# Prompt attention by key-value group: probabilities and values as high and low parts, value products on the full array in place of fp32 products on 64 columns

## The chip, the cores and the metric

One core of a Trainium2 chip runs the whole program. The metric is the device time of one execution in microseconds. Runs of a kernel agree within a few tenths of a per cent most of the time.

## What is computed

One step of a decoder layer: adaLN-modulated norm, one input projection, then a sparse attention (three branches) beside a state-space layer, an output projection and a gated FFN, for a prompt of 1024 tokens and 8 sample sequences of 4 tokens with a cache. The part that matters here is the prompt's attention, by chunks of 128 queries, with 8 query heads of 64 dimensions in two key-value groups of four heads. With 1024 tokens the selected branch keeps all 16 blocks, so it is plain causal attention:

```python
p_c = masked_softmax(s_c, m_c)                                  # compressed keys, at most 64 here
o_c = jnp.einsum('bqgrc,bcgd->bqgrd', p_c.astype(v_cmp.dtype), v_cmp)
...
o_s = jnp.einsum('bqgrn,bqgnd->bqgrd', p_s.astype(v_sel.dtype), ...)   # selected blocks
o_w = jnp.einsum('bqgrw,bwgd->bqgrd', p_w.astype(kv_win.dtype), kv_win[:, :, 1])   # window of 512
o = g[..., 0:1] * o_c + g[..., 1:2] * o_s + g[..., 2:3] * o_w
```

All inputs and outputs are fp32. The kernel gets fp32 accuracy in most of its products from splitting an operand into a high part, rounded to fp32r (a matmul format of its own), and a low part, the difference.

## The kernel before

The program is written as phases that open and close pools of tiles, and a scheduler decides from the data dependences, and from a simulation of its own, in which order each engine's instructions stand. Two tiles of one pool and tag share storage, and a tag's count of buffers says how many can be alive. Of PSUM, the accumulator of TensorE, the attention (`phase_attend`, L1003) holds eight banks: four for scores (tag "s", two of two banks), two for transposes ("t"), one for outputs ("o") and one for filler work ("f").

Stages, by time in the trace: adaLN loads up to 43 us; the input projections in fp32r high and low parts (`project`, L927) up to 251; the sample path, the key compression (L494, L516) and the state scan on VectorE (L1526 to L1529) up to 476; then the prompt attention by chunks in the order 4, 0, 6, 1, 7, 2, 5, 3 up to 967; the output projection (`mix_product`, L1718) up to 1088, with the products of row tiles 8 and 7 already within chunk 5; the FFN (L1800, L1843) to the end.

A chunk has two branches (0: all keys up to the chunk; 1: the window of at most five key tiles), and in each two units of four heads, (0, 1, 4, 5) and (2, 3, 6, 7), so a unit has two heads of each key-value group. `attend_scores` writes a head's scores (L1195, L1196, the mask at L1199), VectorE takes the row maximum (L1203, L1211), ScalarE the exponential (L1205, L1212). `attend_values` goes through the unit's key tiles and calls `pv_tile` for each: four transposes of 128 × 128 into a bank of tag "t" (L1269), one copy out of it, by ScalarE and VectorE in turn (L1271), and one fp32 product for each key-value group with 64 columns of values stationary and 256 columns moving (L1273). A product in fp32 is two instructions. The output of both units lies in one bank (group 0 in partitions 0 to 63, group 1 in the rest). `attend_out` copies it (L1280), transposes it (L1283) and multiplies it with the gates (L1288, L1290, then GpSimd L1291). The compressed branch goes through `pv_tile` twice per chunk with 64 rows of values.

Fillers stand between the units by a table (`PLAN`, `between`, L1029): state-space kernels and outputs, the GLU, the second half of the adaLN, the output weights (`out_weights`). They use the bank "f". The second half of the sample path (`sample_attend`) is taken up by four of its steps at chunk 4. `mix_product` uses bank "f" for the row tiles of `MIX` (8 and 7) and "t", "o", "f" for the others; its tiles come from the pool "wo", which `out_weights` opens at chunk 5. Each row tile has 48 products of 512 columns.

In the sample path `sample_load` keeps eight tiles of the cache (256 columns by four, tag "s_raw"), two runs of four. `ada_block` holds three adaLN weight tiles of 1 MB (four contraction rows by 512 columns); the projection's weights have three pairs of half matrices (tag "bw"). `kv_block` writes the projected values into the tile vst in fp32 by one ScalarE copy.

## Time and profile before

| what | value |
|---|---|
| runs timed | 1857.51, 1838.06, 1839.6 us; median 1839.6 |
| profiled execution | 1847.22 us, of which the span of the instructions is 1845.4 us |
| mean clock granted to TensorE | 0.975 of full speed |
| busy: TensorE, VectorE, ScalarE, GpSimd | 95%, 52%, 34%, 23% of the span |
| memory traffic | 143.88 MB read, 25.46 MB written |

PE is TensorE's matmul side, PEld its loading of stationary operands (which overlaps), DVE is VectorE, ACT ScalarE, POOL GpSimd, SP the engine that issues most DMAs. Busy times are sums of the instructions' durations; matmuls overlap, so a matmul's duration is longer than the distance to the next. A group's "idle before" is the time in which the engine stood still ahead of its instructions, with the instruction that ended it. All stage times below are microseconds from the start of the span.

### The profile page before, as it was taken

How to read it: one execution, taken by the hardware profiler on the slowest of the kernel's cores; microseconds unless marked ns; L12 is line 12 of the kernel's file. 1: busy time of each engine (PE TensorE's matmuls, PEld its weight loads, DVE VectorE, ACT ScalarE, POOL GpSimd, SP SyncE). 2: the span in 40 equal slices, each digit the busy share in tenths (PEclk: the TensorE clock that was granted, in tenths of full speed). 3: DMA queues.
4: the chain of work that ended last, by engine and by line, in shares of the span. 5: the costliest groups of instructions: out<-in, count | busy, mean ns of one | idle time of the engine just before them, and what ended most of it. 6: DMA issues, size and time to landing. Idle time of an engine off the chain costs nothing.

```text
span 1845.4 us, 29371 instructions
## 1 busy us (share of the span) xinstructions
PE 1745.5 (95%) x11546; PEld 1454.5 (79%) x11546; DVE 957.5 (52%) x2310; ACT 631.6 (34%) x1267; POOL 425.4 (23%) x817
## 2 busy tenths in 40 slices
...
GB/s 281 96 105 100 74 138 133 218 142 158 77 143 63 55 142 225 144 53 117 43 57 149 92 92 46 69 23 46 69 24 46 69 23 46 69 24 46 52 46 140
DMA packets 132699, 172.43 MB, mean 93 GB/s; under 512 B 17176, under 2 KB 92312, under 8 KB 132304
## 3 DMA queue, kind: packets, MB, share of 16 engines
...
q14 instruction: 48, 0.39, 0.1%
q10 hardware_dynamic: 128, 0.04, 0.0%
HBM read 143.88 MB, written 25.46 MB: 92 GB/s over the span
## 4 chain that ended last, share of the span: by engine, by line
PE 82%; DVE 8%; DMA 5%; ACT 3%; issue 2%; POOL 1%; SPq 0%; DVEq 0%; ACTq 0%; POOLq 0%
PE gu L1800 18%; PE dn L1843 13%; PE g L1800 5%; PE u L1800 4%; PE cp L516 4%; PE aso L1273 4%; PE as L1195 2%; PE ss L823 2%; PE as L1196 1%; PE q0p L927 1%; PE kv1p L927 1%; PE q1p L927 1%; PE ct L494 1%; PE u1p L927 1%; PE ada L226 1%
## 5 line engine op out<-in xcount | busy, mean ns | idle before, releaser
L1800 PE MATMUL gu<-h2h,wh 128*128 128x352 f32 x704 | 228.1, 324 | 5.0 <-ACT h2h L860 5.0
L1800 PE MATMUL gu<-h2h,wl 128*128 128x352 f32 x704 | 227.4, 323 | 0.0
L1800 PE MATMUL gu<-h2l,wh 128*128 128x352 f32 x704 | 227.0, 323 | 0.0
L1849 DVE TENSOR_TENSOR acc<-acc,dn 128x512 f32<-128x512 f32 x144 | 98.9, 687 | 229.9 <-PE dn L1843 229.9
L1808 POOL TENSOR_TENSOR al<-fa,ah 128x352 fp32r<-128x352 f32 (+1 forms) x66 | 69.5, 1053 | 415.7 <-ACT ah L1807 409.7
L1803 ACT ACTIVATE fa<-gu 128x352 f32<-128x352 f32 x44 | 20.4, 465 | 412.9 <-PE gu L1800 412.9
L1843 PE MATMUL dn<-dh,ah 128*128 128x512 f32 x352 | 141.4, 402 | 3.9 <-DVE fin L1852 3.4
L1843 PE MATMUL dn<-dl,ah 128*128 128x512 f32 x352 | 139.7, 397 | 0.0
L1843 PE MATMUL dn<-dh,al 128*128 128x512 f32 x352 | 139.2, 396 | 0.0
L1800 PEld LDWEIGHTS gu<-h2h,wh 128*128 128x128 f32 x704 | 132.7, 188 | 7.9 <-ACT h2h L860 5.3
L1800 PEld LDWEIGHTS gu<-h2l,wh 128*128 128x128 f32 x704 | 133.2, 189 | 3.8
L1800 PEld LDWEIGHTS gu<-h2h,wl 128*128 128x128 f32 x704 | 132.9, 189 | 3.1
L409 ACT CAST wh<-wr 128x1024 fp32r<-128x1024 f32 x44 | 46.0, 1048 | 151.5 <-PE g L1800 77.0
L1806 DVE TENSOR_TENSOR fa<-fa,gu 128x352 f32<-128x352 f32 x44 | 22.9, 521 | 143.9 <-ACT fa L1803 143.9
L1195 PE MATMUL as<-kst,aqA 128*128 128x320 f32 (+4 forms) x192 | 76.5, 402 | 9.0 <-ACT ap L1212 3.7
L1843 PEld LDWEIGHTS dn<-dh,ah 128*128 128x128 f32 x352 | 66.8, 190 | 22.5 <-ACT wh L409 7.5
L410 DVE TENSOR_TENSOR wl<-wr,wh 128x1024 fp32r<-128x1024 f32 x44 | 58.8, 1339 | 49.0 <-ACT wh L409 49.0
L1843 PEld LDWEIGHTS dn<-dl,ah 128*128 128x128 f32 x352 | 66.7, 189 | 15.9
L1843 PEld LDWEIGHTS dn<-dh,al 128*128 128x128 f32 x352 | 67.0, 190 | 8.4
L1196 PE MATMUL as<-kst,aqB 128*128 128x320 f32 (+4 forms) x192 | 65.6, 346 | 6.3 <-ACT aqB L1158 6.3
L1211 DVE TENSOR_REDUCE asm<-as 128x1 f32<-128x640 f32 (+3 forms) x64 | 58.7, 920 | 19.2 <-PE as L1199 18.4
L1212 ACT ACTIVATE ap<-as,asm 128x640 f32<-128x640 f32 (+3 forms) x64 | 55.9, 874 | 36.0 <-DVE asm L1211 22.6
...
## 6 DMA issues: line engine op xcount, KB each, us to landing
...
```

The costliest lines, as they stand in the source:

```text
L410: self.nc.vector.tensor_tensor(lo, raw, hi.bitcast(F32), op=ALU.subtract)
L516: nc.tensor.matmul(P[:, 256 * ab:256 * ab + 256], w[:, 8 * ab + 2 * j + i, :], x[:, i, :], start=j == 0 and i == 0 and n == 0 and ab == 0, ...
L927: nc.tensor.matmul(p[:, t, :n], h[:, k, tok], ww[:, k % 4, :n], start=m == 0, stop=m == 23)
L1195: nc.tensor.matmul(Sv, qA[:, h, :], kk, start=True, stop=False)
L1196: nc.tensor.matmul(Sv, qB[:, h, :], kk, start=False, stop=not mt)
L1211: nc.vector.tensor_reduce(mx[:, :1], Sv, axis=ax, op=ALU.max, negate=True)
L1212: nc.scalar.activation(Pv, Sv, AF.Exp, bias=mx[:, :1], accum_out=l[:, h:h + 1])
L1273: nc.tensor.matmul(O[64 * g:64 * g + 64, 256 * hf:256 * hf + 256], V[:n, 64 * g:64 * g + 64], pT[:, 256 * g:256 * g + 256], start=first, s ...
L1800: nc.tensor.matmul(gu[i], w[:, k, :], h[:, k, 352 * n:352 * n + 352], start=m == 0, stop=m == 23)
L1808: nc.gpsimd.tensor_tensor(al[:, cols], a[:, :w], ah[:, cols].bitcast(F32), op=ALU.subtract)
L1843: nc.tensor.matmul(p, a[:, sl], w[:, c], start=m == 0, stop=m == 5)
L1849: nc.vector.tensor_tensor(o, o, p, op=ALU.add)
```

## The change

The units of a branch become the two key-value groups (heads 4g to 4g+3) in place of two heads of each. For a unit's key tile `pv_turn` transposes the four heads' probabilities into a bank as before, then copies them as fp32r (high part, ScalarE) and subtracts that from the bank (low part, VectorE). The values are kept as high and low part per group beside each other, 128 columns, so one product of 128 stationary and 512 moving columns gives the product with the high values in one half of the partitions and that with the low values in the other; it is made for the high and for the low probabilities. They are issued two key tiles after the transposes. `pv_join` adds the two halves (a ScalarE copy, a VectorE addition). The compressed branch transposes the probabilities of two heads at once (they share 128 rows), and makes eight products of 256 columns with the values at rows 0 to 63 or 64 to 127 of a tile that is zero elsewhere.

The values' two parts are written by two GpSimd operations for each of eight value blocks (16 in all). PSUM in the attention: four banks "s", three "t", one "o"; the fillers use "t". The pool "wx", which now holds the work tiles of `mix_product`, opens only after the attention's pools are closed. The adaLN weights come in tiles of half the size (four of them, in place of three), the projection's weights in quarter matrices (five pairs, in place of three of halves), the sample path keeps six cache tiles in place of eight, loads them one by one, and writes the next run's scores after the values' products and not before. In `ssm_input` seven more small loads for each of four groups replace a copy.

```diff
-            wt = pool.tile([128, 4, 512], F32, tag="wada", name=f"wada{nb}_{kk}", bufs=3)
-            nc.sync.dma_start(wt, w[:, 4 * kk:4 * kk + 4, nb * 512:(nb + 1) * 512])
+            wts = [pool.tile([128, 2, 512], F32, tag="wada", name=f"wada{nb}_{kk}{i}", bufs=4) for i in range(2)]
+            for i, wt in enumerate(wts):
+                nc.sync.dma_start(wt, w[:, 4 * kk + 2 * i:4 * kk + 2 * i + 2, nb * 512:(nb + 1) * 512])
...
-        self.vst = kv.tile([128, NT, 2, 128], F32, name="vst")
...
+        self.vst = kv.tile([128, NT, 2, 4, 64], F32R, name="vst")
...
-        self.bw = self.open("bw", bufs=3)
+        self.bw = self.open("bw", bufs=5)
...
+            O = self.sample_pv(S, self.raws.pop(run), self.kvn[:, br, 1] if last else None, B, sb, nm)
+            self.own_group(R[br][:, j], O)
+            self.sample_load(sb, 4)
             if half == 0 and k < 4:
                 p = self.sample_scores(runs[k + 1], sb)
-            O = self.sample_pv(S, self.raws.pop(run), self.kvn[:, br, 1] if last else None, B, sb, nm)
-            self.own_group(R[br][:, j], O)
-            self.sample_load(sb)
...
+    def sample_load(self, sb, n):
+
...
+            raw = sb.tile([128, 4, 256], F32, tag="s_raw", name=f"s_raw{br}{b}_{j}", bufs=6)
...
         nm = f"kv{br}_{t2}"
-        vt = pb.tile([128, 2, 128], F32, tag="bk", name=nm + "v") if br == 0 else self.vst[:, 2 * t2:2 * t2 + 2, br - 1, :]
+        vt = pb.tile([128, 2, 128], F32, tag="bk", name=nm + "v")
         nc.scalar.copy(vt, p[:, :, 128:256])
+        if br:
+            v = vt.rearrange("p t (g d) -> p t g d", g=2)
+            slots = self.vst[:, 2 * t2:2 * t2 + 2, br - 1]
+            nc.gpsimd.tensor_copy(slots[:, :, 0:4:3], v)
+            nc.gpsimd.tensor_tensor(slots[:, :, 1:3], v, slots[:, :, 0:4:3].bitcast(F32), op=ALU.subtract)
...
-        self.psum("psc", s=2, t=2, o=1, f=1)
+        self.psum("psc", s=2, t=3, o=1)
...
+        self.wx = self.open("wx", bufs=2)
...
-            tags, self.tags = self.tags, "ff"
+            tags, self.tags = self.tags, self.XT
...
+        self.vch = pc.tile([128, 2, 4, 64], F32R, name="vch", bufs=1)
+        nc.gpsimd.memset(self.vch.bitcast(F32), 0.0)
+        for e in range(2):
+            rows = slice(64 * e, 64 * e + 64)
+            v = self.vcp[rows].rearrange("p (g d) -> p g d", g=2)
+            slots = self.vch[rows, e]
+            nc.gpsimd.tensor_copy(slots[:, 0:4:3], v)
+            nc.gpsimd.tensor_tensor(slots[:, 1:3], v, slots[:, 0:4:3].bitcast(F32), op=ALU.subtract)
...
-        for h in (2 * hf, 2 * hf + 1, 4 + 2 * hf, 5 + 2 * hf):
+        for h in range(4 * grp, 4 * grp + 4):
...
         k0, nk = self.attend_keys(c, br)
-        if hf == 0:
-            st["O"] = self.ps("o", f"aso{c}{br}")
-        O, att, l = st["O"], st["att"], st[br]
+        O, att, l = self.ps("o", f"aso{c}{br}{grp}"), st["att"], st[br]
         g = self.gz[:, c].rearrange("p (h b) -> p b h", b=3)
-        for t in range(nk):
-            self.pv_tile([P[:, t * 128:t * 128 + 128] for P in Ps], self.vst[:, k0 + t, br, :], O, hf, pc, f"as{c}{br}{t}", t == 0, t == nk - 1)
-        st["between"](2 * br + hf)
-        if hf == 0:
+        late = []
+        for t in range(nk + 2):
+            if t < nk:
+                late.append(self.pv_turn([P[:, t * 128:t * 128 + 128] for P in Ps], pc, f"as{c}{br}{grp}{t}"))
+            if t > 1:
+                V = self.vst[:, k0 + t - 2, br, 2 * grp:2 * grp + 2].rearrange("p a d -> p (a d)")
+                for n, x in enumerate(late.pop(0)):
+                    nc.tensor.matmul(O, V, x, start=t == 2 and n == 0, stop=t == nk + 1 and n == 1)
+        if grp == 0:
+            st["ot"] = pc.tile([128, 512], F32, tag="aot", name=f"as{c}{br}ot")
+        self.pv_join(st["ot"], O, grp, pc, f"as{c}{br}{grp}")
+        st["between"](2 * br + grp)
+        if grp == 0:
             return
         nc.vector.reciprocal(l, l)
         nc.vector.tensor_tensor(l, l, g[:, 1 + br], op=ALU.mult)
-        self.attend_out(O, l, att, pc, f"as{c}{br}", br == 0)
+        self.attend_out(st["ot"], l, att, pc, f"as{c}{br}", br == 0)
         if br == 0:
             return
-        O = self.ps("o", f"aco{c}")
-        for i in range(2):
-            self.pv_tile([st["pcb"][:, h, :] for h in (2 * i, 2 * i + 1, 4 + 2 * i, 5 + 2 * i)], self.vcp, O, i, pc, f"ac{c}", True, True)
-        self.attend_out(O, st["lc"], att, pc, f"ac{c}", False)
+
+        pcb = st["pcb"]
+        hl = self.pv_turn([pcb[:, 2 * r:2 * r + 2, :].rearrange("p h n -> p (h n)") for r in range(4)], pc, f"ac{c}")
+        ot = pc.tile([128, 512], F32, tag="aot", name=f"ac{c}ot")
+        for grp in range(2):
+            O = self.ps("o", f"aco{c}{grp}")
+            Ov = O.rearrange("p (r e q) -> p e r q", r=2, e=2)
+            for e in range(2):
+                V = self.vch[:, e, 2 * grp:2 * grp + 2].rearrange("p a d -> p (a d)")
+                for n, x in enumerate(hl):
+                    nc.tensor.matmul(Ov[:, e], V, x[:, 256 * grp:256 * grp + 256].rearrange("p (r q) -> p r q", r=2),
+                                     start=e == 0 and n == 0, stop=e == 1 and n == 1, skip_group_check=True)
+            self.pv_join(ot, O, grp, pc, f"ac{c}{grp}")
+        self.attend_out(ot, st["lc"], att, pc, f"ac{c}", False)
         t = pc.tile([128, 512], F32, tag="aot", name=f"attq{c}")
         self.norm_rows(att.rearrange("p h d -> p (h d)"), t, 1.0, self.xc_d[c * 128:(c + 1) * 128, :512], f"attn{c}", "a")
...

-    def pv_tile(self, Ps, V, O, hf, pc, name, first, last):
-
-        nc = self.nc
-        n = Ps[0].shape[-1]
-        pT = pc.tile([128, 512], F32, tag="apT", name=f"{name}pT{hf}", bufs=3)[:n]
-        p = self.ps_t(f"{name}pt{hf}")[:n]
+    def pv_turn(self, Ps, pc, name):
+
+        nc = self.nc
+        p = self.ps_t(name + "pt")
         for r in range(4):
             nc.tensor.transpose(p[:, r * 128:r * 128 + 128], Ps[r], self.ident)
-        self.flip = not self.flip
-        (nc.scalar.copy if self.flip else nc.vector.tensor_copy)(pT, p)
-        for g in range(2):
-            nc.tensor.matmul(O[64 * g:64 * g + 64, 256 * hf:256 * hf + 256], V[:n, 64 * g:64 * g + 64], pT[:, 256 * g:256 * g + 256],
-                             start=first, stop=last)
-
-    def attend_out(self, O, coef, att, pc, name, first):
-
-        nc = self.nc
-        ot = pc.tile([128, 512], F32, tag="aot", name=name + "ot")
-        nc.scalar.copy(ot, O)
+        h, lo = (pc.tile([128, 512], F32R, tag="apT" + x, name=f"{name}pT{x}", bufs=3) for x in "hl")
+        nc.scalar.copy(h, p)
+        nc.vector.tensor_tensor(lo, p, h.bitcast(F32), op=ALU.subtract)
+        return h, lo
+
+    def pv_join(self, ot, O, grp, pc, name):
+
+        nc = self.nc
+        own, other = slice(64 * grp, 64 * grp + 64), slice(64 - 64 * grp, 128 - 64 * grp)
+        nc.scalar.copy(ot[own], O[other])
+        nc.vector.tensor_tensor(ot[own], ot[own], O[own], op=ALU.add)
+
+    def attend_out(self, ot, coef, att, pc, name, first):
+
+        nc = self.nc
...
-        us = sp.tile([8, 8, 128], F32, tag="q4", name=f"us{Q}")
-        nc.vector.memset(us[:, 0:4], 0.0)
-        nc.sync.dma_start(us[:, 4:8], self.zs_d.rearrange("(b t) f -> b t f", t=4)[:, :, 1304 + 128 * Q:1432 + 128 * Q])
-        ur = sp.tile([128, 8, 8, 16], F32, tag="q4", name=f"ur{Q}")
+        usr = sp.tile([8, 8, 8, 16], F32, tag="q4", name=f"usr{Q}", bufs=3)
+        nc.vector.memset(usr[:, :, 0:4], 0.0)
+        for g in range(8):
+            f = 1304 + 128 * Q + 16 * g
+            nc.sync.dma_start(usr[:, g, 4:8], self.zs_d.rearrange("(b t) f -> b t f", t=4)[:, :, f:f + 16])
...
-            self.g1 = wo.tile([128, 1024], F32, tag="g1", name=f"g1_{tt}", bufs=1)
+            self.g1 = wx.tile([128, 1024], F32, tag="g1", name=f"g1_{tt}", bufs=1)
...
-            p = self.ps("t" if last else "f", f"{nm}xt{k2}")
+            p = self.ps("t", f"{nm}xt{k2}")
...
-            M = self.ps("of"[hf] if last else "f", f"{nm}M{hf}")
+            M = self.ps("ot"[hf], f"{nm}M{hf}")
```

Both kernels' instruction orders on TensorE, at the places that matter. First the middle of a unit of chunk 6, branch 0 in before (as601pT is the transposed tile 1 of that branch, as603pt the bank of tile 3, ap the heads' probabilities, aso the output bank):

```order
L1273 MATMUL aso_8335<-as601pT_8345,vst 64x256 x2
L1269 MATMUL as603pt_8364<-ident,ap_7940 128x128
L1269 MATMUL as603pt_8364<-ident,ap_7950 128x128
L1269 MATMUL as603pt_8364<-ident,ap_7960 128x128
L1269 MATMUL as603pt_8364<-ident,ap_7970 128x128
L1273 MATMUL aso_8335<-as602pT_8354,vst 64x256 x2
```

In the order after the change, the same place (as6002 is tile 2 of the first group, pTh and pTl its high and low part; L1211, L1212 and L1215 write the scores of a head of the next group, as L1195, L1196 and L1199 in before):

```order
L1244 MATMUL aso_8527<-as6002pTh,vst 128x512
L1244 MATMUL aso_8527<-as6002pTl,vst 128x512
L1300 MATMUL as6005pt<-ident,ap_8121 128x128
L1300 MATMUL as6005pt<-ident,ap_8131 128x128
L1300 MATMUL as6005pt<-ident,ap_8141 128x128
L1300 MATMUL as6005pt<-ident,ap_8151 128x128
L1211 MATMUL as_8517<-kst,aqA_8097 128x512
L1212 MATMUL as_8517<-kst,aqB_8098 128x512
L1211 MATMUL as_8517<-kst,aqA_8097 128x384
L1212 MATMUL as_8517<-kst,aqB_8098 128x384
L1215 LDWEIGHTS identb
L1215 MATMUL as_8517<-mk,identb 128x128
```

Two products of 64 columns per turn (one for each group of values) became two of 128 columns (one for each part of the probabilities), and they stand two tiles behind their transposes, with scores of the next group between the turns.

Second, TensorE at the hand-over from the compression to the attention, before (sc, pcT, imp and oc are the sample path's scores, transposed probabilities, importance and output over compressed keys; s240kt to s270kt transposes of cache keys, aqt the transposed queries, as the first scores of chunk 4):

```order
L676 MATMUL sc_6822<-kcT,qblk 32x128 x4
L820 MATMUL s240kt<-ident,s_raw_0_5634 128x128 x4
L820 MATMUL s250kt<-ident,s_raw_0_5636 128x128 x4
L686 MATMUL pcT_6835<-ident,s_pc_6827 128x128
L820 MATMUL s260kt<-ident,s_raw_0_5638 128x128 x4
L1153 MATMUL aqt_6798<-ident,aqhl_6793 128x128 x8
L820 MATMUL s270kt<-ident,s_raw_0_5640 128x128 x4
L691 MATMUL imp_6839<-kc,s_pcT_6837 128x30
L1195 MATMUL as_6957<-kst,aqA_6796 128x320
L695 MATMUL imp_6843<-s_y_6841,kc 128x30
L1196 MATMUL as_6957<-kst,aqB_6797 128x320
L1195 MATMUL as_6957<-kst,aqA_6796 128x320
...
L713 MATMUL oc_6858<-vc,s_pcT_6837 32x128 x4
```

and after (L1211 is the first score, as L1195 in before; sn and ss are scores of the sample path's new and cached keys):

```order
L679 MATMUL sc_6940<-kcT,qblk 32x128 x4
L689 MATMUL pcT_6953<-ident,s_pc_6945 128x128
L694 MATMUL imp_6957<-kc,s_pcT_6955 128x30
L698 MATMUL imp_6961<-s_y_6959,kc 128x30
L716 MATMUL oc_6976<-vc,s_pcT_6955 32x128 x4
L722 MATMUL sn_6985<-knT,qblk 128x64
L820 MATMUL s240kt<-ident,s_raw_0_5717 128x128 x4
L1169 MATMUL aqt_6910<-ident,aqhl_6905 128x128 x8
L823 MATMUL ss_6995<-s240kT,qblk 32x512
L820 MATMUL s250kt<-ident,s_raw_0_5719 128x128 x4
L820 MATMUL s260kt<-ident,s_raw_0_5790 128x128 x4
L1211 MATMUL as_7075<-kst,aqA_6908 128x320
```

The sample path's products from sc to oc stood with other work between them and now stand one behind the other; the transposes of cache keys and queries follow them.

Third, TensorE in chunk 5, before (mx8M is the accumulator of the output projection of row tile 8, woh and wol the parts of its weights, mx8Xh and mx8Xl those of its input):

```order
L1273 MATMUL aso_10849<-as500pT_10850,vst 64x256 x2
L1269 MATMUL as501pt_10860<-ident,ap_10683 128x128
L1269 MATMUL as501pt_10860<-ident,ap_10693 128x128
L1269 MATMUL as501pt_10860<-ident,ap_10703 128x128
L1269 MATMUL as501pt_10860<-ident,ap_10713 128x128
L1269 MATMUL as502pt_10869<-ident,ap_10683 128x128
L1269 MATMUL as502pt_10869<-ident,ap_10693 128x128
L1269 MATMUL as502pt_10869<-ident,ap_10703 128x128
L1269 MATMUL as502pt_10869<-ident,ap_10713 128x128
L1718 MATMUL mx8M_11688<-woh,mx8Xh_11674 32x512
L1718 MATMUL mx8M_11688<-woh,mx8Xl_11675 32x512
L1718 MATMUL mx8M_11688<-wol,mx8Xh_11674 32x512
```

and the first place at which mx8 stands after the change (aco, ac3otp: the compressed branch of chunk 3, the last):

```order
L1266 MATMUL aco_12123<-ac3pTh,vch 128x2x128
L1266 MATMUL aco_12123<-ac3pTl,vch 128x2x128
L1318 MATMUL ac3otp<-ident,ac3ot 128x128 x4
L1741 MATMUL mx8xt_12178<-ident,mx8xc 128x32 x4
L1741 MATMUL mx8xt_12187<-ident,mx8xc 128x32 x4
L1753 MATMUL mx8M_12197<-woh,mx8Xh_12183 32x512
L1753 MATMUL mx8M_12225<-woh,mx8Xh_12183 32x512
L1753 MATMUL mx8M_12197<-woh,mx8Xl_12184 32x512
L1753 MATMUL mx8M_12197<-wol,mx8Xh_12183 32x512
```

The products of row tile 8 stood between the tiles of chunk 5 and now stand behind the last chunk; those of row tile 7 follow them.

## Rows read from the trace of the kernel before

**Rows 1.** The page's first part: busy time and share of the span.
```profile
PE 1745.5 (95%) x11546; PEld 1454.5 (79%) x11546; DVE 957.5 (52%) x2310; ACT 631.6 (34%) x1267; POOL 425.4 (23%) x817
```

**Rows 2.** The page's chain that ended last, shares of the span by engine.
```profile
PE 82%; DVE 8%; DMA 5%; ACT 3%; issue 2%; POOL 1%; SPq 0%; DVEq 0%; ACTq 0%; POOLq 0%
```

**Rows 3.** Windows: length, busy us of PE, PEld, DVE, ACT, POOL, clock, DMA.
```profile
0.00:480.00 480.00, 440.21 (x3492) 380.22 (x3493) 326.27 (x1203) 212.82 (x408) 173.71 (x262) 0.97 0.45 145
480.00:574.30 94.30, 87.04 (x706) 56.69 (x704) 81.30 (x301) 53.39 (x130) 14.60 (x18) 0.96 0.24 76
574.30:697.00 122.70, 105.83 (x995) 73.84 (x994) 69.51 (x128) 56.22 (x134) 48.78 (x86) 0.87 0.38 111
697.00:850.00 153.00, 142.46 (x924) 89.06 (x922) 94.63 (x148) 92.22 (x198) 47.82 (x170) 0.98 0.40 136
850.00:967.00 117.00, 108.42 (x687) 68.72 (x686) 61.01 (x97) 53.03 (x122) 20.28 (x66) 0.99 0.17 58
967.00:1088.00 121.00, 112.40 (x560) 96.38 (x560) 60.26 (x93) 46.62 (x91) 27.73 (x124) 0.96 0.37 120
```
**Rows 4.** TensorE's longest waits, 490 to 990 us: total, times, longest.
```profile
PE Y L1598 <- DMA ssm_W<-K: 5.9, 1, 5.9
```

**Rows 5.** TensorE's timeline in chunk 6: start, duration, instruction.
```profile
600.88 0.66 PE L1269 MATMUL as603pt<-ident,ap 128*128 128x128 f32 x4
601.46 0.65 PE L1273 MATMUL aso<-as602pT,vst 128*64 128x256 f32 x4
...
604.38 0.66 PE L1269 MATMUL as606pt<-ident,ap 128*128 128x128 f32 x4
```

**Rows 6.** TensorE's timeline in the compression, transposes between fp32r products.
```profile
461.66 0.60 PE L494 MATMUL ct<-ident,cxr 128*128 128x128 f32 x4
462.01 0.36 PE L516 MATMUL cp<-cXl,w1hv 128*128 128x256 f32 x1
462.21 0.28 PE L516 MATMUL cp<-cXh,w1lv 128*128 128x256 f32 x1
462.33 0.28 PE L516 MATMUL cp<-cXh,w1hv 128*128 128x256 f32 x1
```

**Rows 7.** TensorE's timeline in the FFN, fp32r products of 512 columns.
```profile
1299.63 0.40 PE L1843 MATMUL dn<-dh,ah 128*128 128x512 f32 x1
1299.86 0.39 PE L1843 MATMUL dn<-dh,al 128*128 128x512 f32 x1
```

**Rows 8.** Windows of one line: L1269 (PE, PEld), L1271 (DVE, ACT), L1280 (ACT).
```profile
476.00:1008.00 532.00, 98.28 (x592) 66.38 (x592) 0.95 0.31 102
...
476.00:1008.00 532.00, 50.74 (x74) 43.16 (x74) 0.95 0.31 102
...
476.00:1008.00 532.00, 14.02 (x24) 0.95 0.31 102
```
**Rows 9.** Groups of instructions, 476 to 1008 us, by shape: busy us, mean ns.
```profile
L1211 DVE TENSOR_REDUCE asm<-as 128x1 f32<-128x640 f32 x40 | 32.7, 819 | 12.8 <-PE as L1199 12.1
...
L1157 DVE CAST aqB<-aqt 64x512 fp32r<-64x512 f32 x16 | 10.9, 684 | 5.3 <-ACT aqA L1156 5.0
...
L1156 ACT CAST aqA<-aqt 128x512 fp32r<-128x512 f32 x16 | 9.4, 586 | 7.4 <-PE aqt L1153 7.3
...
L1158 ACT CAST aqB<-aqt 64x512 fp32r<-64x512 f32 x16 | 9.2, 581 | 4.0 <-DVE aqB L1157 3.6
...
L1123 POOL TENSOR_SCALAR att<-att,attn_y 128x512 f32<-128x512 f32 x8 | 6.1, 760 | 0.8
```

**Rows 10.** Line L499, the compression's subtraction: ns min/median/max, first and last start.
```profile
L499 DVE TENSOR_TENSOR cXl<-ct,cXh x72: 664/691/698, 253.3 to 470.4; 128x512 fp32r<-128x512 f32 x72
```

**Rows 11.** Timeline of the hand-over, the sample path's first and last product.
```profile
477.90 0.66 PE L676 MATMUL sc<-kcT,qblk 128*32 128x128 f32 x8
...
486.49 0.42 PE L713 MATMUL oc<-vc,s_pcT 128*32 128x128 f32 x8
```

71 lines of the change are left out of this document (33 added, 38 removed).

## The prediction, made before the changed kernel had run

> **What bounds the kernel now.** I read the busy times first, then the chain of waits, then the busy times by stage, and only then single timelines. TensorE is busy for 95% of the span, VectorE for 52%, ScalarE for 34% [rows 1], and TensorE holds 82% of the chain that ended last [rows 2]; so over the whole span TensorE bounds. The change touches the prompt attention from 480 to 967 us, so the stages there count: chunk 4 with the tail of the state scan (480 to 574 us), chunks 0 and 6 with the state-space kernels (to 697), chunks 1, 7 and 2 with the GLU and adaLN (to 850), chunks 5 and 3 with the products of row tiles 8 and 7 of the output projection between them (to 967); then the rest of that projection (to 1088). In these stages TensorE is busy for 87.0, 105.8, 142.5 and 108.4 us of 94.3, 122.7, 153.0 and 117.0: about nine tenths. VectorE has 81.3, 69.5, 94.6 and 61.0 us, and its 81.3 of 94.3 (86%) in the first is the highest share it reaches [rows 3]. The longest single wait of TensorE between 490 and 990 us is 5.9 us [rows 4]. So a microsecond taken from TensorE is worth a microsecond only as long as VectorE, which the change loads, keeps under the share that it reached once.
>
> **TensorE, per key tile.** In the steady state four transposes start at 600.88, the value products at 601.46, and the transposes three tiles on at 604.38: 0.58 us for the transposes, and 3.50 / 3 = 1.17 us for a turn of four heads against 128 keys, so 0.58 for the products too [rows 5]. After the change a turn is four transposes and two full-array fp32r products of 512 columns. Four fp32 transposes between fp32r products take 0.35 us until the next product starts (461.66 to 462.01) [rows 6]; a full-array fp32r product of 512 columns takes 0.23 us (1299.63 to 1299.86) [rows 7]. So 0.35 + 2 × 0.23 = 0.81 us, and 0.355 us is saved. The chunks have 66 key tiles over the two branches (10, 2, 12, 4, 13, 6, 11 and 8 in the order of the chunks), two turns each: 132 turns, 47 us. This agrees with the 592 transposes of before: (132 + 16 compressed turns) × 4 [rows 8]. The compressed branch goes from two turns (2.34 us) per chunk to four transposes and eight products of 256 columns at 0.12 us (462.21 to 462.33) [rows 6]: 0.35 + 0.96 = 1.31 us, 8 × 1.03 = 8 us. TensorE gives up 55 us: 8 in the first stage (20 turns and a chunk), 12 in the second (28 and two), 19 in the third (46 and three), 16 in the fourth (38 and two).
>
> The trace shows the saving as the end of a costly alternation: 64-column fp32 products and transposes next to each other take 0.58 us each [rows 5], while the same transposes beside full-array products take 0.35 [rows 6]. The Trainium skill, "TensorEngine Tiling (Array Packing)", section "When to Use Tiling", recommends for at most 64 stationary columns just what is removed, tiles side by side, and "Theoretical Speedup" promises up to twice the rate; its "Key Properties" say that a change of mode drains the engine. By the rule for columns alone the gain would be the 0.58 of the products less the 0.46 of the new ones, 0.12 × 132 = 16 us; the rows say that the transposes get shorter too, and I go by the rows.
>
> **VectorE and ScalarE.** Today the transposed tile is evacuated once, in turn by ScalarE (74 copies, 43.2 us) and VectorE (74, 50.7 us) [rows 8]. After it every tile is copied by ScalarE (high part) and then subtracted by VectorE (low part): 140 of each (132 turns and 8 compressed). A copy of 128 × 512 costs ScalarE 0.586 us, and a subtraction of that size from the accumulator, as the compression has it, 0.69 us on VectorE [rows 9, 10]. The 48 new joins (two for each of three branches of eight chunks) each cost a ScalarE copy of 64 × 512, 0.58, and a VectorE addition, 0.68 by the conversion of that shape [rows 9]; they replace the 24 copies of 14.0 us [rows 8]. VectorE: 140 × 0.69 + 48 × 0.69 − 50.7 = +79 us. ScalarE: 140 × 0.586 + 48 × 0.58 − 43.2 − 14.0 = +53 us. By stage VectorE gets +11, +18, +28 and +21.
>
> **What moves.** (a) The work tiles of the output projection are opened only when the attention's pools are closed, so the products of row tiles 8 and 7 leave the fourth stage, where they fill TensorE between tiles, and stand behind it. They are 96 products of 0.23 us [rows 7], 22 us, and with their transposes 25; VectorE's part of them is about 9.5 us (some 14 instructions at 0.69 or less). At the 93% at which TensorE runs in the next stage [rows 3] they cost 27 us there. (b) At the hand-over from the compression to the attention the sample path's short chain (scores, importance, output: 477.90 to 486.49 us) has transposes and the first scores between its steps in before [rows 11]; in the new order its six products stand one behind the other, each waiting for a small VectorE or ScalarE step, and what filled the 8.6 us comes behind. The price lies between 0 (the rest of the cache path starts no later) and 8.6 us (nothing covers the chain); half of it, 4 us, is taken, since a part of the 8.6 was the fillers' own time. (c) Smaller weight tiles, six cache tiles in place of eight, 16 more GpSimd operations and 28 more small loads lie, but for the adaLN tiles of the third stage, in the first 480 us, where TensorE computes projections and compression. Their cover is TensorE's work, 440 of these 480 us, beside which GpSimd has 174 [rows 3]; without that cover the 16 operations, at 0.76 us or less as a GpSimd operation on 128 × 512 takes [rows 9], would add up to 12 us, and fewer buffers could cost a wait as long as the longest one seen, 5.9 us [rows 4]. I take 0, with −4 to +6. The FFN from 1088 us on keeps its instructions: 0.
>
> **The sum by stage.** First stage: VectorE 81.3 + 11 = 92.3 us against TensorE's 94.3 − 8 = 86; VectorE leads. At 90% of it 102.5 us, the hand-over's 4 included: +8 (0 if VectorE can be full, +14 if it stays at its 86% and the hand-over comes on top). Second: TensorE 122.7 − 12 = 110.7, VectorE 87.5; with 3 us for joins with nothing beside them 113.7: −9 (−12 to −3). Third: TensorE 153 − 19 = 134, VectorE 122.9, which at 86% is 143; I take 145: −8 (−19 to 0, the last at 80%). Fourth: TensorE 117 − 25 − 16 = 76, VectorE 61 + 21 − 9.5 = 73, at 86% 84.5, so −32.5, and the next stage +27: −5.5 (−14 to +8). Together +8 − 9 − 8 − 5.5 = −14.5 us. The profiled execution took 1847.2 us (span 1845.4), so 1832.7; the median of the runs is 1839.6, 0.4% below that execution, and on that scale the forecast is 1826 us. The ends of the four and of the first 480 us, added as if independent, give −17 and +18, so 1809 to 1844 for this case alone.
>
> **Rivals.**
> 1. TensorE alone decides and the saving is had in full: −55 + 4 = −51, 1789 us. For it: 95% busy and 82% of the chain [rows 1, 2], and ScalarE would stay near 75%. Against it: VectorE would need 376 us (92 + 87.5 + 123 + 73) in 487 − 25 − 51 = 411, a share of 91% where its best stage shows 86% [rows 3].
> 2. VectorE's serial place on the transposed bank decides, and it gets slower. A bank is held for transposes 0.35, copy 0.59 and subtraction 0.69, 1.6 us; each time VectorE is in a row maximum (0.82 us for 640 keys [rows 9]) it is 2.4 us, and three banks then give a tile per 0.8 us at best, less whatever the filler work takes, which has lost its own bank and uses these three. VectorE's 376 us need 487 − 27 = 460 us or less for a gain: a share of 82%. Below that it is a loss; at 78% the attention takes 482 us, +22, 1862 us. For it: the shares of 57%, 62% and 52% in stages two to four now [rows 3] are far from 82%. Against it: they are low now because TensorE is the bound. The Trainium skill, "TensorEngine Tiling (Array Packing)", section "PSUM Bottleneck", warns of just this end of it, evacuation taking over once TensorE is faster; no run yet shows it.
> 3. The saving turns into waits at the ends of groups. The products come two tiles late, so at the end of each of 48 groups the last tile waits for 0.59 + 0.69 us, less one product of 0.23: 48 × 1.05 = 50 us if nothing lies beside, −55 + 50 = −5, and 1835 us. Against it: in the new order the next heads' scores stand between a group's turns, so most ends are covered.
> That the change doesn't do what it says (an fp32 product left on the slow path) is ruled out by the new order, which has fp32r operands of 128 × 512 throughout.
>
> **Chances.** The forecast 0.50, rival 1 0.15, rival 2 0.21, rival 3 0.14. A change of 1% (18 us) is about what a measurement of this kernel can tell from none, so faster means below 1821. Of the forecast's case some 40% lies below that: 0.20; with rival 1 and a little of rival 3 0.36. Rival 2 and the upper end of the forecast give 0.21 slower. The rest, 0.43, is within 1%. The range goes to 1795, where most of rival 1 is left out, and to 1857, where half of rival 2 is.
>
> **What would show it.** Right: a period of 0.8 us between the transposes of two tiles in the long chunks; VectorE at 85% or more from 480 to 850 us; TensorE's waits there led by the subtraction and the row maxima; the stage of chunk 4 longer than before, that of chunks 0 and 6 some 9 us shorter; mixing products only behind the last chunk. Wrong: a tile period still over 1 us; VectorE well below 80% with TensorE idle (then the chain of copies and not VectorE's load is the bound); a gain or loss before 480 or after 1088 us of more than 4 us.

## The result: 4.4% slower, and where the time went

The changed kernel takes 1924.4 us (median of 4 runs, 1918.9 to 1924.8), the kernel before, run beside it, 1842.8 (4 runs, 1838.1 to 1857.5): a ratio of 1.044, with 95% from 1.041 to 1.047. The profiled execution took 1924.16 us, with a span of 1922.4, 77.0 us more than the span before. The forecast was 1826 us in a range up to 1857: wrong in sign and outside its range.

The page of the changed kernel, busy times and chain, against [rows 1, 2]:

```profile
PE 1768.4 (92%) x11254; PEld 1496.6 (78%) x11254; DVE 1034.1 (54%) x2433; ACT 679.8 (35%) x1371; POOL 436.0 (23%) x838
...
PE 75%; DVE 9%; DMA 5%; issue 4%; ACT 4%; POOL 3%; SPq 1%; DVEq 0%; ACTq 0%; POOLq 0%
```

TensorE's share fell from 95% to 92%, and its share of the chain that ended last from 82% to 75%; VectorE has 9% of that chain. The busy times by stage, against [rows 3] (stretch, length, busy us of PE, PEld, DVE, ACT and POOL, granted clock, DMA share, GB/s); the rows are chunk 4, chunk 0, chunk 6, chunks 1 and 7, chunk 2, chunks 5 and 3:

```profile
483.00:602.00 119.00, 95.86 (x660) 64.36 (x657) 96.56 (x333) 58.56 (x134) 22.32 (x26) 0.91 0.32 109
602.00:654.00 52.00, 37.86 (x371) 28.33 (x370) 26.39 (x49) 20.38 (x52) 32.02 (x38) 0.76 0.21 50
654.00:741.00 87.00, 76.36 (x619) 57.81 (x618) 59.46 (x106) 51.53 (x120) 17.54 (x62) 0.91 0.40 125
741.00:866.00 125.00, 110.23 (x633) 78.81 (x632) 84.11 (x131) 75.78 (x162) 28.93 (x106) 0.91 0.33 110
866.00:915.00 49.00, 40.50 (x197) 29.43 (x195) 38.01 (x55) 33.81 (x68) 16.70 (x51) 0.81 0.25 82
915.00:1007.90 92.90, 76.31 (x416) 56.54 (x416) 66.30 (x102) 57.06 (x121) 13.38 (x34) 0.90 0.12 37
```

In no stage is any engine full: VectorE has 96.56 of 119 us in chunk 4 (81%), then 62%, 70% and 71% of the other three stages of [rows 3], and TensorE, nine tenths busy before, has 81% to 87%. The granted clock is lower too, lowest (0.76) in chunk 0, where TensorE is busy for the smallest share (37.86 of 52 us). Over the whole attention, before and after:

```profile
478.00:965.00 487.00, 444.20 (x3310) 288.88 (x3311) 306.89 (x680) 254.53 (x582) 130.61 (x338) 0.95 0.31 99
```

```profile
483.00:1008.00 525.00, 437.22 (x2887) 315.37 (x2883) 370.89 (x775) 297.13 (x656) 130.88 (x315) 0.89 0.28 91
```

The attention is 38 us longer, though the products of row tiles 8 and 7 are gone from it, and VectorE has 64 us more. The chunks can be told apart by the ends of the last transposes of each chunk's output. The table gives the distances of these ends on TensorE in us, worked out from those records, for the profiled executions of the kernels that are told of below. "To the scores" ends with the sample path's scores over compressed keys (`sc`), so chunk 4 begins with the hand-over; "to mix" runs from the end of chunk 3 to the first product of row tile 6 of the output projection, "to FFN" from there to the first down product:

| kernel | to the scores | 4 | 0 | 6 | 1 | 7 | 2 | 5 | 3 | to mix | to FFN | FFN |
|---|---|---|---|---|---|---|---|---|---|---|---|---|
| before | 478.6 | 91.7 | 25.5 | 102.7 | 41.5 | 83.5 | 34.1 | 75.2 | 32.5 | 1.3 | 149.3 | 729.6 |
| after | 483.3 | 118.8 | 52.0 | 86.9 | 34.8 | 90.6 | 48.8 | 61.2 | 31.5 | 30.0 | 155.1 | 729.3 |
| e1_fbank | 484.9 | 108.0 | 39.1 | 96.7 | 50.4 | 89.7 | 36.4 | 58.2 | 36.3 | 32.6 | 158.2 | 729.5 |
| e4_before_t3 | 482.9 | 123.9 | 51.0 | 83.7 | 24.1 | 90.9 | 35.6 | 51.0 | 26.6 | 32.1 | 154.9 | 729.4 |
| e10_before_mixt | 481.5 | 94.7 | 24.2 | 99.7 | 41.6 | 81.1 | 33.3 | 51.7 | 29.2 | 30.4 | 158.5 | 729.2 |
| e11_t3_ssb | 473.5 | 109.4 | 46.0 | 88.2 | 23.7 | 89.7 | 35.9 | 51.7 | 26.6 | 30.9 | 155.9 | 729.0 |
| e14_nosub_nojoin | 483.5 | 121.5 | 50.8 | 83.4 | 26.3 | 90.9 | 40.3 | 49.4 | 27.6 | 26.6 | 154.9 | 729.4 |

The first column scatters by some 10 us, between kernels too that are the same up to there. After against before: chunk 4 is 27 us longer; chunks 0 and 6 together 11 longer (their work shifts from one to the other); chunks 1, 7 and 2 are 15 longer; chunks 5 and 3, which lost the products of row tiles 8 and 7, only 15 shorter, while those products now stand behind the attention and cost 29 in "to mix" and 6 behind it. The first of row tile 8, by its tile (ns least, median and most, then first and last start):

```profile
L1753 PE MATMUL mx8M<-woh,mx8Xh x16: 390/396/635, 1008.8 to 1021.6; 128*32 128x512 f32 x16
```

One tile's turn in the long chunk 7, TensorE alone, against [rows 5] (start, duration, instruction):

```profile
807.72 0.60 PE L1300 MATMUL as7012pt<-ident,ap 128*128 128x128 f32 x4
808.07 0.48 PE L1244 MATMUL aso<-as7010pTl,vst 128*128 128x512 f32 x1
808.39 0.60 PE L1300 MATMUL as7013pt<-ident,ap 128*128 128x128 f32 x4
808.74 0.48 PE L1244 MATMUL aso<-as7011pTh,vst 128*128 128x512 f32 x1
809.06 0.49 PE L1244 MATMUL aso<-as7011pTl,vst 128*128 128x512 f32 x1
809.39 0.60 PE L1300 MATMUL as7014pt<-ident,ap 128*128 128x128 f32 x4
809.74 0.48 PE L1244 MATMUL aso<-as7012pTh,vst 128*128 128x512 f32 x1
810.25 0.50 PE L1244 MATMUL aso<-as7012pTl,vst 128*128 128x512 f32 x1
810.59 0.60 PE L1300 MATMUL as7015pt<-ident,ap 128*128 128x128 f32 x4
```

The transposes start at 808.39, 809.39 and 810.59: periods of 1.00 and 1.20 us where 0.81 was forecast and 1.17 stood before. The second has a wait in it: the product at 810.25 reads the low part `as7012pTl`, and VectorE beside it shows when that was ready:

```profile
808.30 0.69 DVE L1303 TENSOR_TENSOR as7011pTl<-as7011pt,as7011pTh 128x512 fp32r<-128x512 f32 x1 [0.36 <-ACT as7011pTh L1302]
808.91 0.68 DVE L1120 SCALAR_TENSOR_TENSOR gl0s<-gl0t,gl0s 128x512 f32<-128x512 f32 x1
809.51 0.69 DVE L1303 TENSOR_TENSOR as7012pTl<-as7012pt,as7012pTh 128x512 fp32r<-128x512 f32 x1
```

The subtraction starts at 809.51 behind an operation of the GLU and takes 0.69 us, to 810.20; the product follows 0.05 us later. The first period isn't free of it either: the low part `as7011pTl` was ready at 808.99, only 0.07 us before its product at 809.06, and that product takes 0.33 us to the next start, where the median behind another product is 0.23.

TensorE's waits in the attention (who waits at which line, for what; us in total, times, longest), against the 5.9 us of [rows 4]:

```profile
PE as L1211 <- ACT ap L1228: 6.1, 9, 1.4
PE as L1211 <- ACT ap L1221: 5.2, 5, 2.1
PE gl7st L1107 <- DVE gl7s L566: 4.4, 1, 4.4
PE aso L1244 <- DVE as10ot L1311: 4.1, 1, 4.1
PE Y L1633 <- DVE y L1641: 3.5, 1, 3.5
PE as L1212 <- ACT aqB L1174: 3.2, 5, 1.2
PE ac2otp L1318 <- DVE ac2ot L1311: 3.0, 1, 3.0
PE ac0otp L1318 <- DVE ac0ot L1311: 2.6, 1, 2.6
PE s111pt L829 <- ACT s_S L756: 2.5, 1, 2.5
```

Summed over all rows of this view, TensorE waits 87 us here and 42 in the kernel before. 30 of the 87 are for the addition of the new join (L1311: 18 by the output transposes L1318, 12 by the value products L1244 and L1266, which want the accumulator back), 7 for the subtraction L1303 and 7 for the copy L1302. The view names direct waits only. It doesn't say what the 87 us are worth, so parts were taken out one by one. Row maxima, which the prediction named beside the subtraction, lead none of the larger waits.

### The profile page after: what moved, and what is told of

Same layout as the page of the kernel before. It is cut to its first block, busy times and chain, and to the rows that moved or that the text cites. A ratio compares the mean times of both kernels' runs of the same rounds, so it can differ in the third digit from the quotient of the medians.

```text
span 1922.4 us, 29211 instructions
## 1 busy us (share of the span) xinstructions
PE 1768.4 (92%) x11254; PEld 1496.6 (78%) x11254; DVE 1034.1 (54%) x2433; ACT 679.8 (35%) x1371; POOL 436.0 (23%) x838
## 4 chain that ended last, share of the span: by engine, by line
PE 75%; DVE 9%; DMA 5%; issue 4%; ACT 4%; POOL 3%; SPq 1%; DVEq 0%; ACTq 0%; POOLq 0%
PE gu L1835 18%; PE dn L1878 12%; PE cp L519 5%; PE g L1835 5%; PE u L1835 4%; PE aso L1244 2%; PE ss L823 2%; PE ct L497 2%; PE ada L228 1%; PE as L1211 1%; PE q0p L928 1%; PE q1p L928 1%; PE as L1212 1%; PE kv0p L928 1%; PE u1p L928 1%
## 5 line engine op out<-in xcount | busy, mean ns | idle before, releaser
L1211 PE MATMUL as<-kst,aqA 128*128 128x320 f32 (+4 forms) x192 | 76.7, 407 | 11.8 <-ACT ap L1228 6.1
L1212 PE MATMUL as<-kst,aqB 128*128 128x320 f32 (+4 forms) x192 | 66.6, 353 | 3.2 <-ACT aqB L1174 3.2
L1835 PE MATMUL g<-h2h,wh 128*128 128x352 f32 x176 | 58.0, 329 | 5.0 <-ACT h2h L860 5.0
(2878 smaller groups left out, 4933.9 us busy)
```

What stands on the lines that cost most here:

```text
L1211: nc.tensor.matmul(Sv, qA[:, h, :], kk, start=True, stop=False)
L1212: nc.tensor.matmul(Sv, qB[:, h, :], kk, start=False, stop=not mt)
L1835: nc.tensor.matmul(gu[i], w[:, k, :], h[:, k, 352 * n:352 * n + 352], start=m == 0, stop=m == 23)
```

## Experiments

The theories at the start, by the letters of the expectations: (A) what costs is the bank plan, in which filler work and cache path have no bank of their own, a side of the change that no term of the forecast priced; (B) the joins at the end of each group hold the one output bank; (C) the two steps that empty each transposed bank set the pace. Ratios are to the kernel before, run on the same chip, with 95% intervals.

**The kernel before with the bank plan of the change.** The old value products stay; only the pools change, and the tags by which fillers, cache path and output projection ask for a bank.

```diff
-        self.psum("psc", s=2, t=2, o=1, f=1)
+        self.psum("psc", s=2, t=3, o=1)
-        self.XT = "ff"
+        self.XT = "tt"
-            tags, self.tags = self.tags, "ff"
+            tags, self.tags = self.tags, "tt"
-            p = self.ps("t" if last else "f", f"{nm}xt{k2}")
+            p = self.ps("t", f"{nm}xt{k2}")
-            M = self.ps("of"[hf] if last else "f", f"{nm}M{hf}")
+            M = self.ps("ot"[hf] if last else "t", f"{nm}M{hf}")
```

> The kernel before with that one part of the change: three transpose banks, no filler bank, fillers, cache path and the products of row tiles 8 and 7 on the shared ones; the value products stay as they were. Theory A expects a large part of the loss here, 1870 to 1890 us, with the cache path's score products one by one. Theories B and C expect 1835 to 1850.

Measured: 1887.9 us, 1.023 (1.018 to 1.028). That is within the range of theory A: 45 of the 82 us are there without a single new value product. Its row in the table has the long chunk 4 (123.9) and chunk 0 (51.0) of the changed kernel, and the 32 us before row tile 6.

**The products of row tiles 8 and 7 alone.** Two ways: their work tiles in a pool that is opened only when the attention's pools are closed (e5), and their banks taken from the attention's own (e10).

```diff
+        self.wx = self.open("wx", bufs=2)
...
-            self.g1 = wo.tile([128, 1024], F32, tag="g1", name=f"g1_{tt}", bufs=1)
+            self.g1 = wx.tile([128, 1024], F32, tag="g1", name=f"g1_{tt}", bufs=1)
...
-            h, l = (wo.tile([128, 4, 128], F32R, tag="X" + n, name=f"{nm}X{n}{k2}")[:, :, :P] for n in "hl")
+            h, l = (wx.tile([128, 4, 128], F32R, tag="X" + n, name=f"{nm}X{n}{k2}")[:, :, :P] for n in "hl")
```

> The kernel before with the work tiles of the output projection in a pool that opens after the attention, so that the products of row tiles 8 and 7 can't fill chunk 5; nothing else. If those products covered waits of TensorE, as the prediction had it, the time goes up by the part of 25 us that the attention can't give back: 1850 to 1858 us. If the attention simply gets shorter by what left it: 1838 to 1846.

Measured: 1842.2 us, 0.999 (0.996 to 1.002). It says nothing on the move: the products still stood in chunk 5, from 861.9 us (860.6 in the kernel before). The likely reason, that this kernel had room for the pool beside the others, isn't shown.

```diff
-            p = self.ps("t" if last else "f", f"{nm}xt{k2}")
+            p = self.ps("t", f"{nm}xt{k2}")
-            M = self.ps("of"[hf] if last else "f", f"{nm}M{hf}")
+            M = self.ps("ot"[hf], f"{nm}M{hf}")
```

> The kernel before with the products of row tiles 8 and 7 on the banks of the transposes and the outputs in place of the filler bank, so that they can't stand between the tiles of chunk 5 and come after chunk 3, as after the change. The prediction's step (25 us of filler moved, 27 us later, and the waits of chunk 5 uncovered) expects 1845 to 1858 us; the three-bank run above moved them too and lost 1 us by it up to their end and 6 us up to the first down product, so from that: 1847 to 1852. Nothing lost: 1839 to 1845.

Measured: 1856.9 us, 1.007 (1.005 to 1.009): 13 us. The products left the attention and came behind chunk 3; chunks 5 and 3 gave back 27 us, the two stages behind took 29 and 9 more. That is the upper end of what the prediction's step expects. In e4 the same move cost less: by its row chunks 5 and 3 are 30 us shorter and the two stages behind 31 and 6 longer, 6 us in all. Chunk 4 is 32 us longer there (91.7 to 123.9) and chunks 0 and 6 7, chunks 1, 7 and 2 are 8 shorter, and the rest is the column that scatters. So chunk 4 is by far the largest part of e4's loss.

**The two new steps of VectorE.** The changed kernel without the subtraction, without the join, and without either.

```diff
-        h, lo = (pc.tile([128, 512], F32R, tag="apT" + x, name=f"{name}pT{x}", bufs=3) for x in "hl")
+        h = pc.tile([128, 512], F32R, tag="apTh", name=f"{name}pTh", bufs=3)
         nc.scalar.copy(h, p)
-        nc.vector.tensor_tensor(lo, p, h.bitcast(F32), op=ALU.subtract)
-        return h, lo
+        return h, h
```

> The changed kernel without the subtraction of the low probabilities: the product with the high part is made twice, so TensorE has the same work, VectorE 140 operations (97 us) less, and a transposed bank is free after one copy. It leaves out the low part of the probabilities. Theory C (evacuation sets the pace) expects 1880 to 1897 us, near or below the three-bank run of the old value products (1888). Theory B (the joins) expects 1905 to 1918, from joins that no longer queue behind subtractions.

Measured: 1907.9 us, 1.035 (1.032 to 1.038), 16.5 us under the changed kernel, in theory B's range.

```diff
-        nc.scalar.copy(ot[own], O[other])
-        nc.vector.tensor_tensor(ot[own], ot[own], O[own], op=ALU.add)
+        nc.scalar.copy(ot[own], O[own])
```

> The changed kernel without the joins' addition: one ScalarE copy of the own half of the output per group, no VectorE addition. It leaves out the products with the low values. Theory B expects the 30 us of waits for the joins gone and some of the clock with them: 1885 to 1900 us. Theory C expects 1910 to 1922.

Measured: 1910.5 us, 1.037 (1.033 to 1.040), 14 us under it, in theory C's range. So neither B nor C holds alone.

> The changed kernel without the subtraction of the low probabilities (the product with the high part is made twice) and without the joins' addition (one copy of the own half): TensorE has all its new work, VectorE less than in before. It leaves out the low probabilities and the products with the low values. If TensorE had given up what the prediction said (55 us), this would lie that far under the three-bank run of the old value products (1888): 1833 to 1845 us. If each product that follows a transpose costs 0.31 us and not 0.23, as the trace after shows, TensorE gives up 10 to 20 us only: 1868 to 1880. If the two removed costs are simply additive (16 and 14 us): 1892 to 1896, so nothing given up.

Both edits together (e14): 1882.5 us, 1.020 (1.018 to 1.023), 42 us under the changed kernel. None of the three expected ranges holds it; the nearest is the one in which TensorE gives up 10 to 20 us. It is 11 us more than 16.5 + 14, about as much as the intervals together leave open. The waits go the same way: without the subtraction TensorE waits 35 us for the joins' addition (30 in the changed kernel), without the join 24 us for the two steps of a transposed bank (14 there).

How the 42 us come about can be read from e14 and the changed kernel, in which TensorE has the same 2878 instructions in the attention. The attention took 490.3 us in e14 and 524.6 in the changed kernel. Of these 34 us 13 are waits (74 to 87 us); the other 22 are busy time of TensorE (415 to 437 us). Its time at the lower of the two levels of its clock (1.2 and 2.4 GHz) rose from 79 to 120 us; half of these 42 us would be 21, so the lower clock may be the reason (an estimate: no run changes the clock alone).

And e14 is only 5 us under e4, which has the same banks and the old products (the intervals of the two overlap). The attention of e4 and of e14:

```profile
483.00:970.00 487.00, 430.89 (x3177) 277.41 (x3177) 299.07 (x659) 248.13 (x566) 123.35 (x308) 0.94 0.29 91
```

```profile
483.50:973.80 490.30, 415.15 (x2882) 299.51 (x2879) 255.80 (x585) 292.33 (x656) 127.03 (x314) 0.92 0.31 97
```

The second took 3 us longer, though it has 16 us less on TensorE (430.89 to 415.15) and 43 less on VectorE. So the saving on TensorE is real and buys almost nothing here: by the sums of the waits, 56 us in e4 became 74 in e14. This step is not the products alone. In e14 ScalarE empties every transposed bank and copies the output after every group (292 us busy, 248 in e4), and TensorE waits 32 us for these copies (22 for those of e4). The units by key-value group, the six cache tiles and the new order of the sample path are in it too; no run takes them apart.

**Why chunk 4 is longer.** The cache path's chain for the sample (four keys' transposes, copy, scores, softmax, transposes, values) runs through chunk 4. Its steps for one run of the cache in e4 (start, duration, instruction; bracketed: idle before it and its releaser):

```profile
547.66 1.04 PE L823 MATMUL ss<-s161kT,qblk 128*32 128x512 f32 x2
548.46 1.04 PE L823 MATMUL ss<-s171kT,qblk 128*32 128x512 f32 x2
551.86 0.66 PE L829 MATMUL s111pt<-ident,s_S 128*128 128x128 f32 x4 [2.35 <-ACT s_S L753]
553.19 1.17 PE L840 MATMUL s111o<-s_raw,s111pT 128*32 128x128 f32 x32 [0.68 <-ACT s111pT L831]
```

and the same steps in the kernel before:

```profile
529.50 1.04 PE L823 MATMUL ss<-s171kT,qblk 128*32 128x512 f32 x2
530.48 0.66 PE L1269 MATMUL as410pt<-ident,ap 128*128 128x128 f32 x4
...
535.22 0.60 PE L829 MATMUL s111pt<-ident,s_S 128*128 128x128 f32 x4
535.75 0.65 PE L1273 MATMUL aso<-as413pT,vst 128*64 128x256 f32 x4
...
538.45 1.08 PE L840 MATMUL s111o<-s_raw,s111pT 128*32 128x128 f32 x32
```

Before, attention turns stand between the last score (529.50), the transposes of the softmax (535.22) and the values (538.45), and the chain's own waits cost nothing. With the banks shared, TensorE has nothing between them and waits 2.35 and 0.68 us; and from the first cache run's values to the fifth's it takes 91.9 us where it took 62.7 (571.7 − 509.0). Two things grew in chunk 4: the time from the starts of the score products (32 columns each) to TensorE's next starts, from 11.2 us before to 27.3 in e4, and TensorE's waits, from 6.6 to 20.2. Together that is nearly the 32 us. So there are two theories of why: the score products, side by side before (two to four at once in most runs of the cache) and one by one after; or the chain, which waits its turn for a bank. First the scores emitted together behind their four transposes, in e4 (e11) and in the changed kernel (e3):

```diff
-            self.sample_keys(raw, b, p[32 * i:32 * i + 32, :], sb, i, f"s{br}{b}{j}")
+        kTs = [self.sample_keys(raw, sb, f"s{br}{4 * half + i}{j}") for i, raw in enumerate(self.raws[run])]
+        for i, kT in enumerate(kTs):
+            self.nc.tensor.matmul(p[32 * i:32 * i + 32, :], self.qblk[:, 4 * half + i, :], kT, start=True, stop=True)
...
```

> The kernel before with three shared transpose banks, as in the run above (1888 us), but with the cache path's four score products of a run written behind its four transposes, so that they can stand side by side again. If the cost of the shared banks in chunk 4 (32 us there) is that these products run one by one, 12 to 18 us come back: 1870 to 1876 us. If it is that the chain of the cache path waits for its banks, 1883 to 1890.

> The changed kernel with the cache path's four score products of a run written behind its four transposes. With the old value products this gave back 23 us (1888 to 1865). The same here if the parts are independent: 1897 to 1905. If the new value products take the gap: 1908 to 1918.

Measured: e11 1865.0 us, 1.012 (1.009 to 1.015), 23 us under e4, of which 14 in chunk 4 (9 are in the stretch that scatters). The time behind the score products fell there by the same 14 us, from 27.3 to 13.1. So in e4 parted products are some 14 of the 32 us, within the 12 to 18 expected of that theory; with the 9 us that scatter the whole is above its range. In the changed kernel (e3) 1919.3, 1.040 (1.037 to 1.043), 5 us under it, just above the range for "the new value products take the gap" and within what the intervals leave open: the time behind the products fell from 26.5 to 17.5, and chunk 4 from 118.8 to 113.6. The same in the kernel before, where the scheduler may still part the products (e16), the same in its first half only (e20), and with a section that keeps the four together in both halves (e17, in the changed kernel e18) or in the first half (e19):

```diff
...
+        with self.tc.tile_critical():
+            for i, kT in enumerate(kTs):
+                self.nc.tensor.matmul(p[32 * i:32 * i + 32, :], self.qblk[:, 4 * half + i, :], kT, start=True, stop=True)
...
```

> The kernel before with the four score products of each run of the cache path kept next to each other on TensorE in both halves of the sample (in before they are in the second half, mostly not in the first). Four products of 32 columns take 0.96 us side by side and 0.97 us each alone, so up to 2.9 us for each of the five runs of the first half that stand alone now, if TensorE bounds there: 1829 to 1838 us. If those 14 us are hidden behind the chain of copies and softmax, or the products have to wait for the last of the four tiles: 1840 to 1850.

> The changed kernel with the same: the four score products of each run kept next to each other in both halves. Writing them behind the transposes gave back only 5 us in the changed kernel, and 23 with the old value products; the scheduler still parted some. If parted products are what cost, 1895 to 1908 us. If in the changed kernel VectorE's queue holds chunk 4 (81% busy there) whatever TensorE does: 1912 to 1922.

Measured: e17 1872.0 us, 1.014 (1.012 to 1.017), with chunk 4 at 125.5 us; e18 1929.2, 1.047 (1.044 to 1.051). Both lie above all expected ranges. In e18 the time from these products' starts to TensorE's next ones fell from 26.5 to 12.1 us, and chunk 4 was 123.5 us all the same. But the section has a price of its own: TensorE stands still ahead of the products that it ties, for 10.3 us in all in e18 and 27.6 in e17, where it waited 0.1 and nothing in the kernels without it. One of these stops in e17:

```profile
543.57 1.06 PE L807 MATMUL ss<-s141kT,qblk 128*32 128x512 f32 x1 [7.97 <-DMA s_raw<-in_cache_kv_slc,idx]
```

The copy of the last key had ended at 534.20 there, and from 537.7 us on VectorE and ScalarE stood still too, so the stop belongs to the section and not to the chain. e17's long chunk 4 is these stops (TensorE waits 34.3 us in it, 6.6 before), and e18 spent on them most of what it saved on the products. The forced runs therefore don't decide between the two theories; e11 does in part.

For the first half alone a flag leaves the products of the second where they were (e19; e20 is the same without the section):

```diff
+        if half == 0:
+            with self.tc.tile_critical():
+                for i, kT in enumerate(kTs):
+                    self.nc.tensor.matmul(p[32 * i:32 * i + 32, :], self.qblk[:, i, :], kT, start=True, stop=True)
...
+        if now:
+            nc.tensor.matmul(out, self.qblk[:, b, :], kT, start=True, stop=True)
```

> The kernel before with the score products written behind the four transposes in both halves, not forced. With three shared banks this gave 9 us before the attention and 14 us in chunk 4; in before chunk 4 had the products side by side already: 1832 to 1840 us. If chunk 4 then loses its order as in the forced run: 1855 to 1872.

> The kernel before with the four score products kept next to each other by force in the first half of the sample only, where they stood apart; the second half, beside chunk 4, as in before. The run with both halves forced was 6 us earlier at the start of the attention and lost 34 us in chunk 4. If the two are independent: 1834 to 1840 us. If the first half's change alone brings the order of chunk 4 into disorder: 1855 or more.

> The same, not forced, in the first half only: 1834 to 1840 us by the gain before the attention; 1841 to 1848 if that gain was the shared banks' own.

Measured: e16 1845.2 us, 1.005 (1.003 to 1.006); e19 1838.1, 1.001 (1.000 to 1.003); e20 1849.5, 1.007 (1.005 to 1.009). Chunk 4 stays at 93.9 to 98.6 us; no version is faster than the kernel before. Only e19 lies in an expected range, and there it equals the kernel before on its chip (1836.6), so the hoped-for gain is absent.

**Does the alternation of transposes and products matter by itself?** Two tiles' transposes first, then both tiles' products, in the kernel before; `pv_tile` hands its products back as a function.

```diff
-        for t in range(nk):
+        for t0 in range(0, nk, 2):
+            late = []
+            for t in range(t0, min(t0 + 2, nk)):
...
+            for x in late:
+                x()
...
-        for g in range(2):
+        def values():
+            for g in range(2):
```

> The kernel before with the transposes of two key tiles written together and then their products, so that transposes and 64-column products alternate half as often. By the trace of before a product behind a transpose starts 0.202 us after it and not 0.109, and a transpose behind a product 0.310 and not 0.260: 0.14 us for a tile less, half of it saved, 0.07 x 132 = 9 us at best: 1832 to 1840. If both transpose banks are then full at once and TensorE waits for the copies: 1845 to 1860.

Measured: 1846.6 us, 1.001 (0.999 to 1.003): no difference, so the 9 us at best didn't come.

**Two repairs.** The fillers get a bank of their own back, which leaves two for the transposes (e1); and the join is done by TensorE, in the turn of the output, with products by a stacked identity (e6).

```diff
-        self.XT = "tt"
+        self.XT = "ff"
...
-        self.psum("psc", s=2, t=3, o=1)
+        self.psum("psc", s=2, t=2, o=1, f=1)
```

> The changed kernel with the filler bank back: two banks for transposes and one for the fillers and the cache path, as before the change, in place of three shared ones. Theory A (the fillers lost their own bank and now take turns with the tiles) expects the cache path's score products side by side again (15 us) and the excess of chunks 0 and 2 (some 25 us) mostly gone: 1880 to 1895 us. Theory B (the joins at the end of each group hold the one output bank and keep TensorE waiting) expects no change, 1915 to 1930. Theory C (the two evacuations of each tile set the pace) expects it worse with two banks, 1925 to 1945.

```diff
...
-            nc.tensor.transpose(p[:, r * 128:r * 128 + 128], ot[:, r * 128:r * 128 + 128], self.ident)
...
+                nc.tensor.matmul(p[:, o:o + 64], ot[g][:, r * 128:r * 128 + 128], self.fold, start=True, stop=True, skip_group_check=True)
```

> The changed kernel without the joins: a group's output bank is copied whole (one ScalarE copy), and the two halves are added by TensorE, in the product that turns the output (a stacked identity in place of the identity). 48 VectorE additions and 24 ScalarE copies go, TensorE gets 8 products of 64 columns for 4 transposes. Theory B expects most of the 30 us of waits for the joins gone: 1890 to 1905 us, with the tile period as it was. Theory C expects a shorter tile period from VectorE's 33 us less, and 1900 to 1912. Theory A expects little, 1912 to 1925.

Measured: e1 1917.1 us, 1.038 (1.033 to 1.043); chunk 4 gave back 11 us and chunk 0 13, but chunk 6 took 10 and chunk 1 16 more. That is theory B's range and not A's. e1 takes the third transpose bank away at the same time, so it doesn't price the shared banks in the changed kernel; the 45 us of e4 are shown beside the old products only. e6 1921.0, 1.040 (1.036 to 1.045): the waits fell from 87 to 67 us, but the turning products took 52 us of TensorE in the attention where the transposes had 17 (from their starts to the next, waits left out). So theory B's 1890 to 1905 didn't come: what the joins had cost in waits, TensorE paid in products.

## Why the prediction was wrong

The account by runs: 1843 us to 1888 by the shared banks (e4; most of it in chunk 4); to 1882 by the new products with all that came with them (e14); to 1924 by subtractions and joins. This holds for parts put in in this order: e12 to e14 and e1 show that the parts act on each other.

- **TensorE per tile, 0.355 us saved, 47 in all: failed.** The 1.17 us of [rows 5] is right, but only where a turn's transposes and products follow one another. In the records of before, at the full clock, the last transpose of a group takes 0.20 us until a value product starts (median of some 50 seen), and 0.03 until other work does (some 65). I multiplied a period made of the dearer kind by all 132 turns. And the new turn isn't 0.81: a full-array product right behind transposes takes 0.316 us to the next start (median of 52 at the full clock), and 0.233 behind another product, so a turn is 0.354 + 0.316 + 0.233 = 0.90. The step from 462.01 to 462.21 against 462.21 to 462.33 in [rows 6] had shown that surcharge. What the turns and compressed tiles of the attention took, waits left out and time at the lower clock counted half, fell from 161 us (e4) to 146 (e14): 15 us, where the forecast had 55 for both. The 16 us that the prediction worked out for columns alone was nearer to the truth than the 47 it went by.
- **Shared banks: not in the sum.** Rival 2 mentions in passing that the fillers lost their bank and sets no price on it. With the old products it was 45 us (e4). I read what the new order moves and priced the hand-over (b) at 4 us. That was right in size: from the sample path's last score to the attention's first TensorE waits 3.4 us, where before it waited for nothing. The missing price lies behind it, in the rest of the cache path all through chunk 4: score products that stand alone, and waits.
- **VectorE's load: right in size, wrong in effect.** Forecast +79; 306.9 to 370.9 with some 9.5 moved out is +74. I made of it a limit on a share (full at 86%). VectorE came to 81% in chunk 4 and 62% to 71% later, and its subtractions and joins cost 42 us (e14 against the changed kernel) all the same: a bank is released, or a low part ready, one step late. 13 of them are waits that the trace names, 22 are TensorE's longer busy time on the same instructions. Rival 2, with a chance of 0.21, had the direction: under a share of 82% it expected a loss, and VectorE came to 71% over the attention (370.89 of 525 us). Rival 3 had this mechanism at the ends of groups and took 50 us for it; it set them against −55, and the −55 was wrong. The Trainium skill, "TensorEngine Tiling (Array Packing)", section "PSUM Bottleneck", warns that the copy out of PSUM may become the bottleneck after a 4× speedup of TensorE. No such speedup is here, and the runs agree in direction only: the new products bought 5 us and the added steps that empty the banks cost 42, with no engine full.
- **The moved products (a):** "27 us there" was right (29 in "to mix"), as was their place only behind the last chunk. The −32.5 before it was wrong: chunks 5 and 3 gave 15, since waits took the freed time; and 6 us came in the stage behind, unforeseen.
- **Chunks 0 and 6, −9, and chunks 1, 7 and 2, −8:** came out at +11 and +15. Chunks 0 and 6 are at 134.7 together in e4 already (128.2 before), so that is mostly the banks. Chunks 1, 7 and 2 have 150.6 in e4 (159.1 before), 157.5 in e14 and 174.2 in the changed kernel: most of the loss there is subtraction and join.
- **Right:** the FFN (−0.3); chunk 4 longer than before, though by 27 instead of 8. The first 480 us came within −4 to +6 (+4.7), but as that column scatters by some 10 us this says little.
- **Signs:** those that the prediction named for being wrong came: tile periods of 1.00 and 1.20 us, VectorE well below 80% from chunk 0 on with TensorE idle.
- **A sum:** chunk 4's range doesn't add up. 92.3 / 0.86 is 107.3 us, with the hand-over's 4 that is +17 and not +14, and 92.3 / 0.9 is 102.5 without the 4. The measured +27 lies outside either way.

Open: in e4 some 14 of chunk 4's 32 us are parted score products (e11); how much of the rest is the chain's wait for banks and how much the order in which TensorE takes its steps, no run parts, and in the changed kernel even the 14 aren't shown. Nor has the lower clock a run of its own: by the records the time at the lower of its two levels in the attention went from 50 us before to 61 in e4, 79 in e14 and 120 in the changed kernel. If all the added 70 us were work at half speed, the lower clock would be 35 of the 77 us (an estimate, and an upper one).
